# Memory projections at three quarters of the attention's pace, gating's first operands traced earlier

## The chip, the cores and the metric

The kernel runs on one core of a Trainium2 chip. The metric is device time in microseconds of one execution. An execution under the hardware profiler gives a trace, from which all views (page, windows, waits, chain, timeline) are taken. The engines are called PE (TensorE), DVE (VectorE), ACT (ScalarE), POOL (GpSimd) and SP (SyncE, which issues most loads and stores); PEld is TensorE's weight load.

## The reference, cut to what matters

One step of a hybrid decoder layer, in fp32, for a prompt of 1024 rows and for 8 samples with 8192 rows of paged cache each. The prompt goes through a mixer of two groups of heads (forgetting attention and a spatial gating unit), cross-attention into 256 memory tokens and a gated MLP; the samples go through the same weights against their caches. The parts that this change moves:

```python
def memory_kv(mem, g_mem, w_ck, w_cv):                 # "the memory's projections", 256 x 1024 each
    mn = rmsnorm(mem, g_mem)
    return mn @ w_ck, mn @ w_cv                        # then split into heads
def sgu_prompt(u, z, w_s, b_s):                        # "gating", chunks of 128 rows, 8 heads of 64
    mixed = einsum('hts,bcshd->bcthd', tril(w_s), zc) + b_s
    return u * mixed
...
xp = xp + merge_heads(fox_prompt(q, k, v, logf), sgu_prompt(u, z, w_s, b_s), g_att_out, g_sgu_out, w_o)
```

Gating's z comes normalised (a factor per row and one per column); its result gets an RMSNorm of its own before the merge. fp32 products of full precision are made as three products of split operands (`gemm3`, L272 to L274).

## The kernel before, in words

The prompt is worked in two halves of 512 rows. `p1` makes all input projections and writes q, k, v, u (`sgu_d`) and z (`zg_d`) to DRAM. Then come, for the first half, attention (`attention(0)`), for the second half attention (`attention(1)`), then for each half the merge, the output projection, cross-attention and the MLP.

Python generators set the order in which instructions are traced; each `yield` gives a rough cost. `mix(main, bg, ratio)` goes through `main`, adds `ratio` times the cost of each step to an account, and takes steps from `bg` as long as the account is positive. A decode generator for the samples is paced by the same costs (`PACE`, L76): one cache step per 12 units in the phase `att0`, one per 26 from the third head pair on (`attx`), one per 11 in `att1`. A cache step gathers a page of keys and of values (L1407, L1469), multiplies and reduces on DVE (L1414, L1415), and makes its value products on PE (L1475). The tracer's scheduler then places the instructions on each engine, and may move one ahead of others whose operands or buffers aren't ready in its own model; on the chip each engine runs its list in order.

`attention(0)` goes through four head pairs, each in two blocks of two row blocks for two heads: 8 score groups per pair, 32 in all (1.8 units each). A score group makes the scores (L798, L800, L802), the row maximum (L804) and the exponential (L805). Two groups later the probabilities are turned on PE (L827) and copied (L834) to a probability tile; after a block come the value products (`values`, L843) and the copy back (L852, L863, L865). The next pair is loaded (`load`, L724 to L731) and set up (`setup`, L741 to L783) in the second block of the pair before. At the last pair `late` (L1839) calls twice into `attention(1)`, whose first pair is thereby loaded and set up.

The filler beside it (`fill`, L1832) first gives `pmem` (L674): the memory's projections, 8 chunks of 5.2 units (24 products of 128 x 512 each, L272 to L274, and an evacuation, L711), with the weights loaded and split four at a time (L249, L235, L236). Then comes `gating(0)` (L618): `wst`, the masked chunk weights (L621, L622); for each of two pairs of row blocks the loads of z and u (L629, L630), z scaled (L632), 8 products on PE (L640), bias and product with u on DVE (L650), sums of squares on ACT (L661, which the profile shows at L230); then a reciprocal root (L663, shown at L222 and L223), the scaling (L669) and the store (L670). Each step of it is one unit.

One thing is scarce. `U` (L111) is a set of 18 buffers of 4 KB per partition, which holds all operands of attention, projections and gating: `pmem` keeps 4 (`mh`, `ml`), a head pair of the first half 5 (keys and values as loaded, and two tiles for each head), of the second half 7, gating 5 (`wst`, two z, two u), the probability tiles of a second block 2, attention's result 2. For the part that the change touches:

Of the kernel before, what the change touches and what calls it, by code (L numbers as in the profile page):

```python
# [49 lines left out]

NKV = 4
VLAG = 2
MIXR = 1.0
G0R = 0.0
WH = 5
WL = 4
WR = 4
# [21 lines left out]
def build(nc, tc, ctx, a, phases=None):  # L79
# [46 lines left out]
    def sm(shape, tag, bufs=2, dt=F32):  # L126
        return small.tile(shape, dt, tag=tag, bufs=bufs, name=nm(tag))
# [490 lines left out]
    def gating(hf):  # L618
        gsv = gains[0]
        wst = U([P, 8, P])  # L620
        nc.sync.dma_start(wst, a["wsT"])  # L621
        nc.vector.tensor_tensor(wst, wst, tri.unsqueeze(1).broadcast_to((P, 8, P)), op=ALU.mult)  # L622
        us_, ssu = [], sm([P, 4], "ssu", 1)
        for pr_ in range(2):
            z = U([P, 2, 512])
            u = U([P, 2, 512])
            t0 = hf * 4 + pr_ * 2
            rows = slice(t0 * P, (t0 + 2) * P)
            nc.sync.dma_start(z, zg_d[rows, :].rearrange("(c p) d -> p c d", p=P))  # L629
            nc.sync.dma_start(u, sgu_d[rows, :].rearrange("(c p) d -> p c d", p=P))  # L630
            for i in range(2):
                nc.vector.scalar_tensor_tensor(  # L632
                    z[:, i, :], z[:, i, :], rz[:, t0 + i : t0 + i + 1], gsv, op0=ALU.mult, op1=ALU.mult
                )
            yield 1
            for q in range(2):
                ps = BK()
                for j in range(4):
                    h = q * 4 + j
                    mmul(  # L640
                        ps[:, j * P : (j + 1) * P].rearrange("p (c d) -> p c d", d=64),
                        wst[:, h, :],
                        z[:, :, h * 64 : (h + 1) * 64],
                        start=True,
                        stop=True,
                    )
                for j in range(4):
                    h = q * 4 + j
                    uh = u[:, :, h * 64 : (h + 1) * 64]
                    nc.vector.scalar_tensor_tensor(  # L650
                        uh,
                        ps[:, j * P : (j + 1) * P].rearrange("p (c d) -> p c d", d=64),
                        gp[:, B_S + h : B_S + h + 1],
                        uh,
                        op0=ALU.add,
                        op1=ALU.mult,
                    )
                yield 1
            for i in range(2):
                with tc.issue_after(lastexp[0]) if lastexp else nullcontext():  # L660
                    ssq_into(ssu[:, pr_ * 2 + i : pr_ * 2 + i + 1], u[:, i, :])  # L661
            us_.append(u)
        r = rstd_of(ssu, AW, 4, "r4")  # L663
        yield 1
        for pr_ in range(2):
            u = us_[pr_]
            t0 = hf * 4 + pr_ * 2
            for i in range(2):
                nc.vector.tensor_scalar(u[:, i, :], u[:, i, :], r[:, pr_ * 2 + i : pr_ * 2 + i + 1], None, op0=ALU.mult)  # L669
            nc.sync.dma_start(sgn_d[t0 * P : (t0 + 2) * P, :].rearrange("(c p) d -> p c d", p=P), u)  # L670
        yield 1


    def pmem():  # L674
        rm = const.tile([P, 2], F32, tag="rm", name="rm")
        ssm = sm([P, 2], "ssm", 1)
        for mt in range(2):
            t = U([P, D])
            nc.sync.dma_start(t, a["mem"][mt * P : (mt + 1) * P, :])
            ssq_into(ssm[:, mt : mt + 1], t)  # L680
        r = rstd_of(ssm, D, 2, "r2")
        nc.vector.tensor_copy(rm, r)
        mh, ml = [], []
        for q in range(2):
            h, l = U([P, 4, 256], F32R), U([P, 4, 256], F32R)
            raw = WRAW(1024).rearrange("p (k m) -> p k m", m=256)
            nc.sync.dma_start(raw, a["memT"][q * 512 : (q + 1) * 512, :].rearrange("(k p) m -> p k m", p=P))
            for k in range(4):
                kk = q * 4 + k
                split(raw[:, k, :], h[:, k, :], l[:, k, :], scale=gp[:, G_MEM + kk : G_MEM + kk + 1])  # L690
            mh.append(h)
            ml.append(l)
        ahead = [wraw(wpair(a["w_ck"], kk, 0, 512), 1024) for kk in range(4)]
        before = newest(ENG.Activation)
        yield 0.1
        for w, dst in ((a["w_ck"], mk_d), (a["w_cv"], mv_d)):
            for n in range(2):
                with tc.issue_after(before):
                    ws = [wload(wpair(w, kk, n * 512, 512), 1024, ahead.pop(0) if ahead else None) for kk in range(4)]
                for mt in range(2):  # L700
                    ps = MM()
                    ms_ = slice(mt * P, (mt + 1) * P)
                    gemm3(
                        ps[:, :512],
                        [
                            (mh[k // 4][:, k % 4, ms_], ml[k // 4][:, k % 4, ms_], ws[k // 2][0][:, k % 2, :], ws[k // 2][1][:, k % 2, :])
                            for k in range(8)
                        ],
                    )
                    t = T2()  # L710
                    nc.scalar.activation(t, ps[:, :512], AF.Copy, scale=rm[:, mt : mt + 1])  # L711
                    nc.scalar.dma_start(dst[mt * P : (mt + 1) * P, n * 512 : (n + 1) * 512], t)
                    paused[0] = False
                    yield 5.2
# [1095 lines left out]
    def mix(main, bg, ratio):  # L1810

        t, more, res = 0.0, True, None
        while True:
            try:
                d = next(main)
            except StopIteration as e:
                res = e.value
                break
            yield d
            t += d * ratio  # L1820
            while more and t > 0:
                d = next(bg, None)
                more = d is not None
                if more:
                    t -= d
                    yield d
        if more:
            yield from bg
        return res

    def prompt():
        def fill():  # L1832
            yield from pmem()
            if not G0R:
                yield from gating(0)

        got, ahead = [], []
        att1 = attention(1, lambda: got.append(merge_in(0)))
        att0, fill0 = attention(0, (lambda: next(att1)) if LT < 4 else None, LT), fill()  # L1839

        def early():
            next(att0)
            next(fill0)

        yield from p1(early)
        phase[0] = "att0"
        att = yield from mix(att0, fill0, MIXR)
        def load_x(hf):
            xt = []
            for i in range(4):  # L1850
                t = U([P, D])
                nc.sync.dma_start(t, a["x"][(hf * 4 + i) * P : (hf * 4 + i + 1) * P, :])
                xt.append(t)
            return xt

        if LT > 3:
            yield next(att1)
        ending = close(0, att)
        next(ending)
        phase[0] = "att1"  # L1860
        ba_pool(True)
        if G0R:
            att = yield from mix(gating(0), att1, 1 / G0R)
        else:
            att = yield from beside(att1, ending, (0, 2))
        ba_pool(False)
        ending = close(1, att)
        next(ending)
        ends = []
        for hf in range(2):  # L1870
            if not got and hf == 0:
                got.append(merge_in(hf))
            xt = []
            phase[0] = f"mid{hf}"
            if hf == 0:
                mh, ml = yield from beside(merge(*got.pop()), ending, (3, 7))
            else:
                mh, ml = yield from ahead[0]
            if ends:
                yield from ends.pop()  # L1880
            sq = yield from out_proj(a["w_o"], mh, ml, xt, partial(load_x, hf))
            if hf == 0:
                ys = yield from mix(cross(xt, sq), gating(1), 0.05)
            else:
                ys = yield from cross(xt, sq)
            phase[0] = f"ffn{hf}"
            sq = yield from ffn(hf, xt, ys, (lambda: ahead.append(merge(*merge_in(1))) or ahead[0]) if hf == 0 else None)
            held[0] = False
            ends.append(final(hf, xt, sq))
        yield from ends.pop()  # L1890
# [121 lines left out]
```

## Time and profile before

| | us |
|---|---|
| median of 3 runs | 1818.56 (1815.97 to 1819.52) |
| profiled execution, its time | 1820.56 |
| its span in the trace | 1818.4 |
| PE busy | 1745.0 (96%) |
| DVE busy | 1397.5 (77%) |
| ACT busy | 734.4 (40%) |
| POOL busy | 510.0 (28%) |
| mean granted clock of TensorE | 0.986 of full speed |
| stage: first half's attention, projections, gating | 262.0 to 376.8 |

A window row gives the window, its length, the busy time of PE, PEld, DVE, ACT and POOL in it with instruction counts, the granted clock, the DMA engines' share and GB/s. A timeline row gives start, duration, engine, line, operation, output and inputs, and in brackets the idle time before it and what ended that. A wait row gives who waited for whom, total, times and the longest. A row of the chain gives start, duration and what the time went to. A row of a group gives line, engine, operation, operands and count, then busy time and the mean in ns of one, then idle time before them.

### The profile page before, as it was taken

The numbers are of one execution on the slowest core, as the hardware profiler recorded it, in microseconds if no ns is written. First come the engines' busy times: TensorE is split into PE (matmuls) and PEld (weight loads), VectorE is DVE, ScalarE is ACT, GpSimd is POOL, SyncE is SP. The second block draws the span as 40 slices with busy tenths as digits, with TensorE's granted clock in tenths as the row PEclk, the third lists the DMA queues.
The fourth block names the chain that finished last, engine by engine and source line by source line (L and its number), as shares of the span: only waits on it lengthen the run. The fifth ranks groups of instructions, "written<-read, shape, count | busy, mean of one in ns | idle before, by whom it ended". The sixth has DMA issues, their size and how long they took to land.

```text
span 1818.4 us, 25090 instructions
## 1 busy us (share of the span) xinstructions
PE 1745.0 (96%) x9637; PEld 1294.9 (71%) x9637; DVE 1397.5 (77%) x1729; ACT 734.4 (40%) x1378; POOL 510.0 (28%) x461
## 2 busy tenths in 40 slices
PE   8999999888998999999999999989899999999997
PEld 5887776656676767777777776766576778767775
DVE  4689668888788877999989899898875549845344
ACT  6332365455643544433333244235353324332332
POOL 1252334332133432223332333334222111011110
PEclk9999999899999999999999999989999999999999
DMA  8886889777696986679878779988787777568982
GB/s 295 306 297 231 302 297 329 242 266 224 219 398 257 342 310 260 257 285 340 316 279 311 271 306 340 381 300 324 290 309 290 267 268 265 179 266 289 359 314 82
DMA packets 157074, 521.06 MB, mean 287 GB/s; under 512 B 20874, under 2 KB 40842, under 8 KB 124186
## 3 DMA queue, kind: packets, MB, share of 16 engines
q0 software_dynamic: 57168, 341.14, 49.5%
q1 hardware_dynamic: 92874, 165.73, 26.4%
q10 hardware_dynamic: 6912, 12.59, 1.8%
q8 instruction: 76, 1.25, 0.3%
q14 instruction: 44, 0.36, 0.1%
HBM read 495.47 MB, written 23.93 MB: 286 GB/s over the span
## 4 chain that ended last, share of the span: by engine, by line
PE 72%; DMA 10%; issue 7%; DVE 6%; ACT 2%; POOL 2%; SPq 0%; POOLq 0%; DVEq 0%; ACTq 0%
PE ba L272 11%; PE ba L274 11%; PE ba L273 11%; PE bb L272 5%; PE bb L273 5%; PE bb L274 5%; PE dv L1475 5%; DMA kv<-cache_k,io 3%; DMA wr<-w_in 2%; DMA kv<-cache_v,io 1%; PE dv L321 1%; PE dv L1751 1%; PE ba L1056 1%; PE ba L1055 1%; PE ba L1057 1%
## 5 line engine op out<-in xcount | busy, mean ns | idle before, releaser
L235 ACT ACTIVATE wh<-wr 128x1024 fp32r<-128x1024 f32 (+2 forms) x220 | 228.9, 1044 | 489.2 <-PE ba L273 156.0
L236 DVE TENSOR_TENSOR wl<-wr,wh 128x1024 fp32r<-128x1024 f32 (+2 forms) x220 | 262.5, 1200 | 175.6 <-PE ba L274 65.7
L1407 POOL DMA_INDIRECT kv<-cache_k,io x128 | 205.6, 1606 | 551.2 <-DVE s L1427 318.9
L1423 DVE TENSOR_TENSOR kv<-kv,d 128x1024 f32<-128x1024 f32 (+1 forms) x156 | 258.0, 1681 | 35.1 <-DMA kv<-cache_k,io 35.1
L1427 DVE TENSOR_REDUCE s<-kv 128x16 f32<-128x1024 f32 (+1 forms) x156 | 258.2, 1674 | 0.1
L1469 POOL DMA_INDIRECT kv<-cache_v,io x128 | 165.3, 1291 | 282.8 <-PE dv L1475 191.8
L272 PE MATMUL ba<-u,wh 128*128 128x512 f32 (+1 forms) x560 | 220.3, 395 | 1.7 <-ACT u L238 1.7
L273 PE MATMUL ba<-u,wh 128*128 128x512 f32 (+1 forms) x560 | 220.2, 393 | 1.7 <-DVE u L239 1.5
L274 PE MATMUL ba<-u,wl 128*128 128x512 f32 (+1 forms) x560 | 219.5, 393 | 0.0
L272 PE MATMUL ba<-wh,u 128*128 128x512 f32 (+1 forms) x495 | 186.9, 379 | 0.9 <-ACT u L235 0.9
L273 PE MATMUL ba<-wl,u 128*128 128x512 f32 (+1 forms) x495 | 185.4, 375 | 1.2 <-DVE wl L236 1.2
L274 PE MATMUL ba<-wh,u 128*128 128x512 f32 (+1 forms) x495 | 183.8, 376 | 0.0
L272 PEld LDWEIGHTS ba<-u,wh 128*128 128x128 f32 x560 | 106.8, 191 | 30.6 <-issue 5.6
L273 PE MATMUL bb<-u,wh 128*128 128x512 f32 (+1 forms) x304 | 119.4, 393 | 9.2 <-DVE u L239 9.2
L274 PEld LDWEIGHTS ba<-u,wl 128*128 128x128 f32 x560 | 106.9, 191 | 29.1 <-issue 6.1
L273 PEld LDWEIGHTS ba<-u,wh 128*128 128x128 f32 x560 | 106.7, 191 | 27.5 <-issue 2.7
L1475 PE MATMUL dv<-kv,s 128*32 128x512 f32 x1024 | 124.2, 598 | 1.8 <-DMA kv<-cache_v,io 1.8
L272 PE MATMUL bb<-u,wh 128*128 128x512 f32 (+1 forms) x304 | 119.4, 393 | 0.0
L274 PE MATMUL bb<-u,wl 128*128 128x512 f32 (+1 forms) x304 | 118.6, 390 | 0.0
L272 PEld LDWEIGHTS ba<-wh,u 128*128 128x128 f32 x495 | 93.0, 188 | 26.0 <-issue 6.9
L274 PEld LDWEIGHTS ba<-wh,u 128*128 128x128 f32 x495 | 92.8, 188 | 21.5 <-issue 3.7
L273 PEld LDWEIGHTS ba<-wl,u 128*128 128x128 f32 x495 | 93.1, 188 | 19.7 <-DVE wl L236 1.9
(425 smaller groups left out, 3255.9 us busy)
## 6 DMA issues: line engine op xcount, KB each, us to landing
wr<-w_up SPq DMA_DIRECT2D x88, 512.0 KB
kv<-w_up POOLq DMA_DIRECT2D x22, 1024.0 KB, 8.0
wr<-w_down SPq DMA_DIRECT2D x40, 512.0 KB
kv<-w_down POOLq DMA_DIRECT2D x11, 1024.0 KB, 8.5
wr<-w_in SPq DMA_DIRECT2D x16, 512.0 KB
wr<-w_o SPq DMA_DIRECT2D x16, 512.0 KB
wr<-w_cq SPq DMA_DIRECT2D x16, 512.0 KB
wr<-w_co SPq DMA_DIRECT2D x16, 512.0 KB
```

The costliest lines, as they stand in the source:

```text
L235: nc.scalar.activation(h, src, AF.Copy)
L236: nc.vector.tensor_tensor(l, src, h.bitcast(F32), op=ALU.subtract)
L272: mmul(out, sh, mh, start=(i == 0), stop=False)
L273: mmul(out, sh, ml, start=False, stop=False)
L274: mmul(out, sl, mh, start=False, stop=(i == n - 1))
L321: mmul(ps[32 * j : 32 * j + 32, :w], xT[:, k, :] if nk == 8 else xT[:, k * 8 : k * 8 + 32], raw[:, q, j * w : (j + 1) * w], start=(k == 0) ...
L1055: mmul(pss[i], mh[k][:, tb], wh, start=(k == korder[0]), stop=False)
L1407: nc.gpsimd.indirect_dma_start(kv, None, a["cache_k"], off(kidx[:, b, ch : ch + 1]))
L1423: nc.vector.tensor_tensor(kvv[:, i : i + m, :], kvv[:, i : i + m, :], qb.unsqueeze(1).broadcast_to((P, m, 512)), op=ALU.mult)
L1427: nc.vector.tensor_reduce(s[:, ch * 4 + i : ch * 4 + i + m, :].rearrange("p k h -> p (k h)"), kvv[:, i : i + m, :].rearrange("p k (h d) -> ...
L1469: nc.gpsimd.indirect_dma_start(kv, None, a["cache_v"], off(kidx[:, b, ch : ch + 1]))
L1475: mmul(dv[32 * j : 32 * j + 32, :], s[:, ch * 4 : ch * 4 + 4, :].rearrange("p k h -> p (k h)"), kvv[:, j, :], start=(ch == 1), stop=(ch == ...
```

## The change

`MIXR` goes from 1.0 to 0.75, so that `mix` takes 0.75 units of filler for each unit of attention. `gating` is cut otherwise: loading and scaling a pair's operands becomes `inputs(pr_)`; the first pair's is traced with `wst` as its first step, the second pair's directly ahead of that pair's products, without a step between. `fill` takes that first step out of `gating(0)` after the seventh step of `pmem`, that is with two projection chunks still to come, and the rest after `pmem`'s end. The switch `G0R`, which was 0, is taken out with its branches. `gating(1)`, used beside cross-attention, gets the same new cut. Nothing is computed differently.

```diff
-MIXR = 1.0
-G0R = 0.0
+MIXR = 0.75
...
-        us_, ssu = [], sm([P, 4], "ssu", 1)
-        for pr_ in range(2):
+        ssu = sm([P, 4], "ssu", 1)
+        us_, zs_ = [], []
+        def inputs(pr_):
             z = U([P, 2, 512])
             u = U([P, 2, 512])
...
                 nc.vector.scalar_tensor_tensor(
                     z[:, i, :], z[:, i, :], rz[:, t0 + i : t0 + i + 1], gsv, op0=ALU.mult, op1=ALU.mult
                 )
-            yield 1
+            us_.append(u)
+            zs_.append(z)
+
+        inputs(0)
+        yield 1
+        for pr_ in range(2):
+            if pr_ == 1:
+                inputs(1)
+            z, u = zs_[pr_], us_[pr_]
             for q in range(2):
...
-            us_.append(u)
         r = rstd_of(ssu, AW, 4, "r4")
...
         def fill():
-            yield from pmem()
-            if not G0R:
-                yield from gating(0)
+            gate, n = gating(0), 0
+            for t in pmem():
+                n += 1
+                yield t
+                if n == 7:
+                    yield next(gate)
+            yield from gate
...
-        if G0R:
-            att = yield from mix(gating(0), att1, 1 / G0R)
-        else:
-            att = yield from beside(att1, ending, (0, 2))
+        att = yield from beside(att1, ending, (0, 2))
```

## The prediction

> **What bounds the kernel now.** I read the page first. TensorE is busy nearly throughout, so an edit can only gain where TensorE idles or runs below full clock. Then the table of windows, cut at the change's stage:
>
> ```profile
> PE 1745.0 (96%) x9637; PEld 1294.9 (71%) x9637; DVE 1397.5 (77%) x1729; ACT 734.4 (40%) x1378; POOL 510.0 (28%) x461
> ```
>
> ```profile
> 262.00:333.60 71.60, 69.89 (x387) 51.53 (x387) 60.45 (x101) 41.07 (x88) 28.95 (x35) 1.00 0.83 298
> 333.60:342.80 9.20, 7.04 (x52) 5.32 (x50) 6.28 (x16) 3.27 (x11) 3.18 (x5) 1.00 1.03 400
> 342.80:347.20 4.40, 0.04 (x1) 0.04 (x1) 2.80 (x9) 2.06 (x7) 0.00 (x0) 0.92 0.56 174
> 347.20:353.40 6.20, 6.20 (x29) 5.89 (x30) 4.37 (x11) 1.55 (x3) 1.21 (x2) 0.51 0.14 42
> 353.40:376.80 23.40, 18.56 (x127) 12.26 (x126) 19.23 (x42) 16.03 (x47) 12.63 (x18) 0.93 0.83 266
> ```
>
> The first half's attention begins at 262.0 us, the last memory projection ends at 333.6, the second half's attention starts at 376.8. The columns are length, busy time of PE, PEld, DVE, ACT and POOL, then granted clock, DMA share and GB/s. With projections beside it (first row) attention leaves TensorE idle for 71.6 - 69.9 = 1.7 us. After them, in 43.2 us, TensorE is busy for 7.04 + 0.04 + 6.20 + 18.56 = 31.8, idle for 11.4; 4.4 of these are one gap, after which the clock is 0.51 for 6.2 us (3.0 us lost) and 0.93 in the rest (0.07 x 18.56 = 1.3 lost).
>
> The list of TensorE's waits names the gap, and the chain of waits says what lies behind it:
>
> ```profile
> PE bb L640 <- DVE u L632: 4.4, 1, 4.4
> PE ba L640 <- DVE u L632: 0.6, 1, 0.6
> ```
>
> ```profile
> 295.66 18.74 DMA u<-o_k
> 330.81 14.86 DMA u<-zg_d
> 359.66 2.01 DMA ks_d<-u
> 366.29 9.43 DMA sgn_d<-u
> ```
>
> The long wait is for gating's **second** operands: z of its second pair of row blocks, issued at 330.8 and landed 14.9 us later. The **first** operands, those that the change brings forward, cost 0.6 us.
>
> **What decides when a load may go out.** The 18 buffers of `U` are all taken here. I compared issue times with the ends of earlier users:
>
> ```profile
> 315.17 0.39 PE L800 MATMUL ba<-u,u 68*128 68x512 f32 x1
> 326.37 0.40 PE L800 MATMUL ba<-u,u 68*128 68x512 f32 x1
> ```
>
> ```profile
> 315.62 0.34 SPq L621 DMA_DIRECT2D u<-wsT  x1
> 316.02 0.43 SPq L629 DMA_DIRECT2D u<-zg_d  x1
> 326.81 0.37 SPq L630 DMA_DIRECT2D u<-sgu_d  x1
> 327.35 0.37 SPq L730 DMA_DIRECT2D u<-o_k  x1
> 330.81 0.37 SPq L629 DMA_DIRECT2D u<-zg_d  x1
> ```
>
> ```profile
> 333.87 0.56 POOL L750 DMA_DIRECT2D u<-cq_d  x1 [4.12 <-PE bb L274]
> 368.45 0.56 POOL L762 DMA_DIRECT2D u<-ck_d  x1 [0.39 <-PE ms L843]
> 380.21 0.54 POOL L750 DMA_DIRECT2D u<-cq_d  x1 [8.12 <-DMA sgn_d<-u]
> ```
>
> A pair of buffers falls free when a head's last scores end (315.5, 326.8); `wst` with the first z go out at once at the first, the first u with the next head pair's keys at the second. The second z goes at 330.8, halfway through the last projection chunk, when half of its `mh` and `ml` are done with. Counting buffers in program order (4 of the projections, 2 results, 5 per head pair, 1 per probability tile, 5 of gating) gives 18 at each of these points, and every release goes to the request that is next in program order. So I take it that buffers are handed out in the order of the program, though the loads themselves are ready long before.
>
> **The change, part by part.** Counted from the code, attention has 74.6 units of work, projections 41.6, gating 8 (after: 7). At ratio 1 the last projection chunk comes after 16 of 32 score groups, at 0.75 after 22.
>
> *More cover.* In the trace 14 score groups run after the projections:
>
> ```profile
> L798 PE MATMUL ba<-u,u 128*128 128x384 f32 (+3 forms) x14 | 6.2, 444 | 0.0
> ```
>
> Their loss without the gap and its slow clock is 11.4 - 4.4 + 1.3 = 8.3 us, 0.6 each. After the change 10 are left: 4 x 0.6 = 2.4 us less; the covered stretch grows by four groups at its own loss of 2.4% (1.7 of 71.6), about 0.3. **Gain 2.1.**
>
> *The gap at its present place* goes, as the second operands are now traced in the last head pair: 4.4 + 3.0 = **7.4**. The first operands' 0.6 lies in the 8.3 already. Their three SP issues, 1.1 us in the rows above, are moved ahead of the second half of w_cv on SP. Those weights went out 27.9 us ahead of use, which covers it:
>
> ```profile
> 289.88 5.60 SPq L249 DMA_DIRECT2D wr<-w_cv  x4
> ```
>
> ```profile
> 317.77 0.48 PE L272 MATMUL ba<-wh,u 128*128 128x512 f32 x1
> ```
>
> If that cover went, the 10.4 us for which SP stood at L630 would be the price.
>
> *What is late next.* In the changed program the second half's set-up (`late`, called at the last head pair's start) asks for 7 buffers before `inputs(1)` asks for 2. Ahead of the second z then stand one buffer of the last head pair's set-up, 2 probability tiles and these 7: 10. Until the last head pair the releases are 2 (the third pair's first head), 4 (projections), 2 (its second head) and 1 (the first z): 9. So the second z and u wait for the next release, the third head pair's last `values` (L843), which also released L762 above. Here is that point beside the last pair's first and last scores, and the second attention's first probability tile:
>
> ```profile
> 360.49 0.46 PE L798 MATMUL ba<-u,u 128*128 128x128 f32 x1
> 366.62 1.73 PE L843 MATMUL ms<-u,u 128*64 128x256 f32 x14
> 372.47 0.48 PE L798 MATMUL ba<-u,u 128*128 128x512 f32 x1
> 384.64 0.59 ACT L834 ACTIVATE u<-bb 128x512 f32<-128x512 f32 x1
> ```
>
> I call the first of these S. `values` ends at S + 7.9, attention's scores at S + 12.5, the second attention's first probability tile is written at S + 24.1. Gating's chain from there needs these rows:
>
> ```profile
> 340.41 2.05 PE L640 MATMUL ba<-u,u 128*128 128x128 f32 x16 [0.57 <-DVE u L632]
> ```
>
> ```profile
> L632 DVE SCALAR_TENSOR_TENSOR u<-u,rz,xg 128x512 f32<-128x512 f32 x4 | 2.8, 746 | 1.6 <-DMA u<-zg_d 1.6
> L650 DVE SCALAR_TENSOR_TENSOR u<-bb,gp,u 128x128 f32<-128x128 f32 x4 | 1.1, 345 | 0.8 <-PE bb L640 0.8
> L230 ACT ACTIVATE junk<-u 128x512 bf16<-128x512 f32 x4 | 2.5, 626 | 0.0
> L230 ACT ACTIVATION_READ_ACCUMULATOR junk<-u 128x1 f32 x4 | 0.8, 193 | 0.0
> L223 POOL TENSOR_TENSOR r4r<-r4r,mhalf 128x4 f32<-128x4 f32 x1 | 1.0, 1045 | 0.1
> L669 DVE TENSOR_SCALAR u<-u,r4r 128x512 f32<-128x512 f32 x4 | 1.7, 479 | 0.0
> ```
>
> The load's landing isn't known for the new time: between 2.0 (`ks_d`) and 18.7 (`o_k`). I take 9.4, that of `sgn_d`, also 512 KB from SP and in the same uncovered stretch; the same for the store at the end. Then S + 7.9 + 9.4 + 2 x 0.75 (L632) + 2.05 (L640) + 4 x 0.345 (L650) + 2 x 0.82 (squares) + 1.0 (POOL; the small DVE step left out) + 1.7 (L669) + 9.4 (store) = S + 36.0. By the same count the buffers of the second attention's first probability tiles come from this store (before, its next head pair waited for it, 380.21 above). Behind ACT's waiting L834 stand its exponentials, and TensorE waits for those. The entry is 36.0 - 24.1 = **11.9 later** against S. For a slow clock after a gap of this kind I add half of 3.0, **1.5**, since set-up transposes may break the gap; the bounds are 0 and 3.0.
>
> *Decode.* Fewer units come before the pace falls from one step per 12 to one per 26: 7.43 steps instead of 8.0.
>
> ```profile
> L1475 PE MATMUL dv<-kv,s 128*32 128x512 f32 x1024 | 124.2, 598 | 1.8 <-DMA kv<-cache_v,io 1.8
> ```
>
> A step has 124.2 / 128 = 0.97 us of TensorE; 0.57 of one moves into later, fuller stages: **+0.6** (0 if it meets idle time).
>
> **Sum:** -2.1 - 7.4 + 11.9 + 1.5 + 0.6 = **+4.5 us**. The profiled execution took 1820.56 us (span 1818.4), the runs' median is 1818.56 (1815.97 to 1819.52), so I apply it to the median: **1823**. With both transfers at 2.0 the entry is no later and the sum is -8.9; with both at 18.7 it is some 23. One of the two at the 14.9 of the second z, or as much sooner than 9.4, gives this case's own range, 1817.5 to 1828.5.
>
> [...] After the gap of 4.4 us the row shows a clock of 0.51. [...]
>
> **The rivals.** *Second operands in time:* buffers are handed to whoever is ready, and the second z goes out when the last projection's four buffers fall free, well ahead of use. Then nothing runs late: -2.1 - 7.4 + 0.6 = -8.9, of which I keep -7 because the covered stretch holds more attention for DVE: **1811.5**. For it: the loads have no other condition, and traffic is thinner once projections are spread. Against: `wst` waited until 315.6 although it was ready. It decides if the second z lands before the last head pair's second score group.
>
> *The gap only moves:* the operands are late, but probability tiles get other buffers. The gap costs 7.4 at its new place as at the old one: -2.1 + 0.6 = -1.5, **1817**. That would also be the case that the change doesn't do what it says for the time: sooner first operands meet a wait of 0.6 us.
>
> **How the numbers follow.** Forecast 44%, operands in time 34%, the gap moves 22%. Faster by over 0.2% (3.6 us, about what a measurement of this kernel can tell from no change) takes 32 of the second case and 3 of the third: 0.35. Slower takes 40 of the first and 3 of the third: 0.43. Same is the rest, 0.22. The range 1809 to 1829 covers the second case down to -8.9 and the first case's own range, and leaves out its ends with two slow or two fast transfers and a gain in the second case beyond its sum.
>
> **What would show it.** Right: in the changed profile the second `zg_d` load goes out after the last `values` of the third head pair, L640's wait stands among the last scores or behind them, and L834 at the second attention's start waits for the `sgn_d` store. Wrong: the second `zg_d` load goes out as the projections end and L640 doesn't wait; or L834 goes ahead of the store. The cover is shown by fewer than 14 score groups after the last projection. Decode's gathers would run half a step later from there on.

## The result and the profile after

The changed kernel takes **1827.17 us** (median of 6 runs, 1824.74 to 1828.37) against 1817.31 (6 runs, 1814.22 to 1819.52) for the kernel before: ratio **1.0057**, 95% interval 1.0044 to 1.0070. It is slower by 9.9 us. The profiled execution took 1828.13 us, its span is 1826.4, 8.0 longer than before.

The lines of the changed kernel stand up to 8 away from those of the kernel before: gating's products are L648 (L640 before), the split products L271 to L273, scores L805 (L798), turning L834 (L827), the copy to a probability tile L841 (L834), `values` L850 (L843), the split copies L238 (L239), decode's key multiply L1430 (L1423).

Page, busy time by engine: TensorE makes the same 9637 products and is busy as long (1744.6 against 1745.0), and the mean clock is the same (0.985 against 0.986). So the 8 us are idle time on the whole, though single stretches run slower or faster than before.

```profile
PE 1744.6 (96%) x9637; PEld 1293.3 (71%) x9637; DVE 1396.4 (76%) x1725; ACT 737.3 (40%) x1380; POOL 489.9 (27%) x461
```

The windows of the changed stage. The last projection ends at 348.6, the last head pair's first scores (the prediction's S) begin at 352.35, the second attention at 382.61:

```profile
261.30:348.60 87.30, 81.70 (x449) 59.07 (x448) 67.54 (x113) 49.07 (x112) 36.82 (x47) 0.98 0.80 280
348.60:354.00 5.40, 5.26 (x43) 4.53 (x41) 4.62 (x14) 4.16 (x10) 1.67 (x3) 1.00 0.80 261
354.00:358.80 4.80, 0.00 (x1) 0.03 (x1) 4.56 (x9) 2.67 (x9) 2.20 (x4) 0.84 0.90 289
358.80:364.00 5.20, 4.32 (x19) 2.06 (x19) 0.65 (x3) 0.38 (x1) 0.52 (x1) 0.50 0.03 11
364.00:369.04 5.04, 0.00 (x1) 0.00 (x1) 1.42 (x2) 0.38 (x1) 0.00 (x0) 0.50 0.76 237
369.04:374.00 4.96, 4.96 (x24) 4.87 (x25) 2.05 (x8) 0.28 (x1) 0.00 (x0) 0.50 0.01 3
374.00:382.70 8.70, 7.62 (x50) 4.80 (x49) 6.98 (x20) 8.03 (x25) 2.27 (x3) 0.98 0.21 62
```

Where before there was one gap of 4.4 us with 6.2 us at a clock of 0.51 behind it, there are now two, of 4.8 and 5.0, and TensorE's 4.32 + 4.96 = 9.3 us of work behind them all run at 0.50. TensorE's waits in 340:392 name both gaps:

```profile
PE bb L648 <- DVE u L632: 5.0, 1, 5.0
PE ms L1454 <- DVE pm L1448: 4.8, 1, 4.8
```

The first is gating's wait for its second operands, at its new place. The second was not there before: decode's softmax (L1448, L1454) comes due ahead of the third head pair's `values`, and DVE, whose reduction it waits for, is busy for 4.56 of these 4.80 us. The timeline says how the one leads to the other:

```profile
356.19 0.46 ACT L812 ACTIVATE t<-ba,mx 128x256 f32<-128x256 f32 x1
358.80 0.37 PE L1454 MATMUL ms<-cp,pm 128*8 128x128 f32 x1 [4.82 <-DVE pm L1448]
359.54 3.26 PE L850 MATMUL ms<-u,u 128*64 128x256 f32 x16 [0.37 <-DVE m L1457]
363.09 0.52 POOL L769 DMA_DIRECT2D u<-ck_d  x1 [6.84 <-PE ms L850]
363.39 0.54 SPq L629 DMA_DIRECT2D u<-zg_d  x1
364.02 0.42 SPq L630 DMA_DIRECT2D u<-sgu_d  x1
367.57 1.42 DVE L632 SCALAR_TENSOR_TENSOR u<-u,rz,xg 128x512 f32<-128x512 f32 x2 [7.65 <-DMA u<-zg_d]
369.04 2.08 PE L648 MATMUL bb<-u,u 128*128 128x128 f32 x8 [5.04 <-DVE u L632]
370.91 0.42 PE L834 MATMUL bb<-cp,t 128*128 128x128 f32 x1
372.69 0.45 PE L805 MATMUL ba<-u,u 128*128 128x128 f32 x1
383.16 1.15 SPq L677 DMA_DIRECT2D sgn_d<-u  x2
390.39 0.60 ACT L841 ACTIVATE u<-bb 128x512 f32<-128x512 f32 x1 [0.93 <-issue]
```

`values` ends at 359.54 + 3.26 = 362.8, and only then do L769, the second z and the second u go out. The z has landed by 367.57, some 4.2 us after its issue. L648 waits 5.04 us for it and starts at 369.04, and what follows on TensorE starts behind it: a turning (L834, at 370.91) of probabilities that were written by 356.7, and the last pair's remaining scores (from 372.69).

**The lag along the kernel.** To see where 8 us come from I compared the start of the same instruction in both traces (changed minus before): the second attention's first scores, and the first product of each of the four output projections (L1055 in the kernel before: the mixer's and cross-attention's, for each half), then the last split product. All kernels of this study, one profiled execution each:

| us later than before at | second attention | mixer's output, half 1 | cross's output, half 1 | mixer's output, half 2 | cross's output, half 2 | last product | median, ratio |
|---|---|---|---|---|---|---|---|
| kernel before, time | 376.9 | 497.1 | 651.8 | 1135.3 | 1295.5 | 1808.7 | |
| after | +5.8 | +5.7 | +15.4 | +18.8 | +9.9 | +8.0 | 1.0057 |
| A ratio alone | +13.3 | +11.2 | +16.3 | +15.4 | +11.8 | +11.2 | 1.0091 |
| B cut alone | -8.6 | -5.9 | +9.2 | +7.8 | +7.0 | +7.9 | 1.0078 |
| C second operands sooner | -3.4 | -0.3 | +8.5 | +8.9 | +1.5 | +1.8 | 1.0047 |
| D old cut in half 2 | +7.2 | +6.4 | +16.5 | +14.8 | +8.0 | +6.5 | 1.0099 |
| E after, decode ahead | +4.7 | +5.3 | +9.0 | +18.1 | +11.9 | +10.8 | 1.0111 |
| F before, decode behind | -1.6 | -0.7 | +0.2 | +3.3 | +11.8 | +9.4 | 1.0081 |
| G B, one unit | -8.1 | -2.5 | +0.9 | +11.0 | +21.7 | +18.8 | 1.0081 |
| H C, decode ahead | -0.9 | +2.1 | +5.6 | +8.9 | +5.0 | +5.3 | 1.0049 |
| I cut of half 1, old account | -8.4 | -8.2 | -12.0 | -13.7 | -14.1 | -14.1 | 0.9955 |
| J I with the ratio | +5.6 | +6.8 | +3.0 | +4.6 | +2.3 | +2.4 | 1.0025 |

Two things limit what the table can say. E has the changed kernel's program up to the second attention, F that of the kernel before, G that of B and H that of C, and their starts there differ from those by 1.1, 1.6, 0.5 and 2.5 us; so a difference of a stage under some 3 us says nothing. And the last column is not the ratio: the profiled execution of the kernel before took 3.2 us more than the median of its runs, D's 7.5 less than that of its own, those of E and F 3.7 less, G's 3.8 more.

In the changed kernel the entry costs 5.8, the first half's middle stage another 9.7 (5.7 to 15.4), and the second half's gives 8.9 back (18.8 to 9.9). My prediction had the first of these only. In the first half's cross-attention TensorE's waits (552:602) hold

```profile
PE bb L272 <- DVE u L238: 8.4, 3, 6.5
```

against, at the same place in the kernel before (545:597),

```profile
PE bb L273 <- DVE u L239: 3.2, 3, 2.1
```

That is 5.2 of the 9.7 us. DVE's timeline shows what stands ahead of the copies that TensorE waits for: a multiply of decode's keys, for whose page DVE waits 1.90 us:

```profile
559.97 0.87 DVE L238 SCALAR_TENSOR_TENSOR u<-ba,gp,u 128x256 fp32r<-128x256 f32 x2
562.75 2.36 DVE L1430 TENSOR_TENSOR kv<-kv,d 128x1024 f32<-128x1024 f32 x2 [1.90 <-DMA kv<-cache_k,io]
565.02 0.48 DVE L238 SCALAR_TENSOR_TENSOR u<-ba,gp,u 128x256 fp32r<-128x256 f32 x1
```

So two theories stood after the result. **Entry:** buffers are handed out in program order, the second operands come late, and the rest is a consequence of the time of arrival. **Decode's place:** both the ratio and the new cut change how many units pass before each pace sets in, so decode's steps fall elsewhere in the later stages, and that moves the time by itself.

### The profile page after: what moved, and what is told of

Read it like the earlier page. It is cut to its first block, busy times and chain, and to the rows that moved or that the text cites. A ratio compares the mean times of both kernels' runs of the same rounds, so it can differ in the third digit from the quotient of the medians.

```text
span 1826.4 us, 25085 instructions
## 1 busy us (share of the span) xinstructions
PE 1744.6 (96%) x9637; PEld 1293.3 (71%) x9637; DVE 1396.4 (76%) x1725; ACT 737.3 (40%) x1380; POOL 489.9 (27%) x461
## 4 chain that ended last, share of the span: by engine, by line
PE 62%; issue 5%; DMA 4%; DVE 3%; ACT 2%; POOL 1%; POOLq 0%; DVEq 0%; ACTq 0%; SPq 0%
PE ba L271 9%; PE ba L272 9%; PE ba L273 9%; PE bb L273 5%; PE bb L272 5%; PE bb L271 5%; PE dv L1482 5%; DMA kv<-cache_v,io 1%; PE dv L320 1%; PE dv L1758 1%; DMA kv<-cache_k,io 1%; DMA u<-an_d 1%; PE ba L1062 1%; PE ba L1064 1%; PE ba L1063 1%
## 5 line engine op out<-in xcount | busy, mean ns | idle before, releaser
L235 DVE TENSOR_TENSOR wl<-wr,wh 128x1024 fp32r<-128x1024 f32 (+2 forms) x220 | 262.2, 1199 | 156.1 <-PE ba L273 62.4
L1414 POOL DMA_INDIRECT kv<-cache_k,io x128 | 176.1, 1376 | 593.3 <-DVE s L1434 397.7
L1430 DVE TENSOR_TENSOR kv<-kv,d 128x1024 f32<-128x1024 f32 (+1 forms) x158 | 260.5, 1677 | 36.3 <-DMA kv<-cache_k,io 36.3
L1476 POOL DMA_INDIRECT kv<-cache_v,io x128 | 170.1, 1329 | 279.8 <-PE dv L1482 219.9
L271 PE MATMUL ba<-u,wh 128*128 128x512 f32 (+1 forms) x560 | 220.0, 394 | 4.0 <-ACT u L237 3.3
L272 PE MATMUL ba<-u,wh 128*128 128x512 f32 (+1 forms) x560 | 219.5, 392 | 1.7 <-DVE u L238 1.7
L273 PE MATMUL ba<-u,wl 128*128 128x512 f32 (+1 forms) x560 | 218.4, 391 | 0.0
L271 PE MATMUL ba<-wh,u 128*128 128x512 f32 (+1 forms) x495 | 187.0, 380 | 2.9 <-ACT u L234 1.7
L272 PE MATMUL ba<-wl,u 128*128 128x512 f32 (+1 forms) x495 | 186.2, 377 | 1.7 <-DVE wl L235 1.7
L273 PE MATMUL ba<-wh,u 128*128 128x512 f32 (+1 forms) x495 | 184.1, 377 | 0.0
L271 PEld LDWEIGHTS ba<-u,wh 128*128 128x128 f32 x560 | 105.9, 189 | 34.9 <-issue 7.3
L272 PE MATMUL bb<-u,wh 128*128 128x512 f32 (+1 forms) x304 | 118.5, 390 | 12.7 <-DVE u L238 12.7
L272 PEld LDWEIGHTS ba<-u,wh 128*128 128x128 f32 x560 | 106.0, 189 | 34.1 <-issue 9.4
L273 PEld LDWEIGHTS ba<-u,wl 128*128 128x128 f32 x560 | 106.0, 189 | 28.1 <-issue 5.2
L271 PE MATMUL bb<-u,wh 128*128 128x512 f32 (+1 forms) x304 | 118.2, 389 | 0.5 <-ACT u L237 0.5
L273 PE MATMUL bb<-u,wl 128*128 128x512 f32 (+1 forms) x304 | 117.7, 388 | 0.0
L271 PEld LDWEIGHTS ba<-wh,u 128*128 128x128 f32 x495 | 93.3, 189 | 27.7 <-issue 6.9
L272 PEld LDWEIGHTS ba<-wl,u 128*128 128x128 f32 x495 | 93.5, 189 | 20.2 <-DVE wl L235 2.8
L273 PEld LDWEIGHTS ba<-wh,u 128*128 128x128 f32 x495 | 93.1, 189 | 20.6 <-issue 3.7
```

The lines of the kernel that those rows point to most:

```text
L235: nc.vector.tensor_tensor(l, src, h.bitcast(F32), op=ALU.subtract)
L271: mmul(out, sh, mh, start=(i == 0), stop=False)
L272: mmul(out, sh, ml, start=False, stop=False)
L273: mmul(out, sl, mh, start=False, stop=(i == n - 1))
L1414: nc.gpsimd.indirect_dma_start(kv, None, a["cache_k"], off(kidx[:, b, ch : ch + 1]))
L1430: nc.vector.tensor_tensor(kvv[:, i : i + m, :], kvv[:, i : i + m, :], qb.unsqueeze(1).broadcast_to((P, m, 512)), op=ALU.mult)
```

## The experiments

Ratios are to runs of the kernel before on the same chip. Edits are made in the changed kernel where nothing else is said. "Account" is the sum of units that decode's pace draws on.

**A and B: each part alone.** A is the kernel before with the new ratio, B the changed kernel with the old one.

```diff
-MIXR = 1.0
+MIXR = 0.75
```

> The kernel before with the ratio 0.75 alone (gating and its place as before, all after the last projection chunk). Theory (the last head pair's set-up of the second half takes the buffers that gating's second operands need, and gating's end runs into the second attention): gating is now traced wholly behind the last projection, so its second z goes out later still; a wait at L640 of 4 to 8 us and a start of the second attention 4 to 8 us after that of the kernel before; total 1821 to 1830. Rival (the new cut of gating is what costs): no wait longer than before, total 1812 to 1818.

A: 1833.38 us (1828.60 to 1838.34), ratio 1.0091 (1.0068 to 1.0114). The waits are as long as expected, but there are two, and the start and the time lie beyond the range. With all of gating behind the projections, both operands are waited for, and between the two requests lie 19 us (SP's issues, then TensorE's waits, of A):

```profile
349.55 0.43 SPq L629 DMA_DIRECT2D u<-zg_d  x1
368.64 0.53 SPq L629 DMA_DIRECT2D u<-zg_d  x1
```

```profile
PE ba L640 <- DVE u L632: 5.4, 1, 5.4
PE bb L640 <- DVE u L632: 4.7, 1, 4.7
```

> The changed kernel with the ratio back at 1.0: new cut of gating and its first step two chunks before the projections' end. Theory: projections end before the last two head pairs, their four buffers come free well before the second half's set-up asks, so the second z goes out about 331 us as before and the wait stays near 4.4 us; the second attention starts within 2 us of the kernel before; total 1814 to 1822. Rival (the cut costs): about the changed kernel's 1827.

B: 1829.48 us, ratio 1.0078 (1.0056 to 1.0100). The time is the rival's. Its second z goes out during the projections, as expected, but no wait of gating's for it follows, and the second attention starts 8.6 us sooner than before:

```profile
332.81 0.37 SPq L629 DMA_DIRECT2D u<-zg_d  x1
```

So the new cut gains at the entry, which I had not expected, and the ratio loses there: it alone makes the entry 13.3 late, and beside the cut it moves it from 8.6 sooner to 5.8 later. But B is slower than the kernel before all the same: it loses 15 us between the mixer's output and cross's output of half 1 (-5.9 to +9.2). Entry alone can't be the reason.

**C: the second operands asked for when gating resumes,** ahead of `late`'s seven requests.

```diff
         inputs(0)
         yield 1
+        if hf == 0:
+            inputs(1)
         for pr_ in range(2):
-            if pr_ == 1:
+            if pr_ == 1 and hf:
                 inputs(1)
```

> The changed kernel with the first half's second operands requested when gating resumes after the projections, ahead of the second half's set-up; gating of the second half as changed. Theory (buffers are handed out in program order): the second z goes out as the projections end, about 349 us, and not after the third head pair's last value products (363.4 in the changed kernel); the wait at L648 falls from 5.0 to under 1 us, the second attention starts 5 to 9 us sooner than in the changed kernel. Total 1816 to 1822 if the rest stays, since 2 to 10 us of the loss lie in cross-attention of the first half. Rival (the stall is the decode's softmax before it, a wait of 4.8 us on DVE): the start moves by under 2 us.

C: 1824.49 us (11 runs, 1819.05 to 1830.50), ratio 1.0047 (1.0033 to 1.0062). SP's issue and TensorE's longest wait there, of C:

```profile
345.56 0.37 SPq L629 DMA_DIRECT2D u<-zg_d  x1
```

```profile
PE bb L650 <- ACT junk L229: 3.9, 1, 3.9
```

Only the place in the program changed, and the second z goes out 17.8 us sooner (363.39 in the changed kernel), as an order of buffers by the program would have it. The wait for z is gone, the other wait (decode's softmax) too, with gating's products now ahead of it in TensorE's list (357.44 and 361.26), and one of 3.9 is left. The second attention starts 9.2 sooner than in the changed kernel. The time hardly falls, and misses the expected range: the ratio is 1.0047 against 1.0057, with overlapping intervals. This kernel too loses 9 us behind the mixer's output.

**D: the old cut in the second half's gating,** which is worked beside cross-attention.

```diff
-        inputs(0)
-        yield 1
+        if hf == 0:
+            inputs(0)
+            yield 1
         for pr_ in range(2):
-            if pr_ == 1:
+            if hf:
+                inputs(pr_)
+                yield 1
+            elif pr_ == 1:
                 inputs(1)
```

> The changed kernel with the old cut for the second half's gating alone, which runs beside cross-attention of the first half. Theory A (the loss of some 10 us in cross-attention of the first half comes from where decode's DVE work meets the turning of the rows, not from gating's cut): total within 3 us of the changed kernel's 1827, or any change comes with another position of decode. Theory B (the new cut costs there): the wait of 6.5 us at the turning goes, total 1817 to 1820.

D: 1834.17 us, ratio 1.0099 (1.0076 to 1.0122), slower than the range of either theory; it also gives decode back the unit of the second half's cut. The loss in the middle stage stays (+6.4 to +16.5), and so does the wait at L272 (8.3, the longest 6.4): in this kernel it isn't due to gating's new cut beside cross-attention.

**E to H: decode moved by itself.** Going through the generators with the paces shows that at the first half's middle stage decode is 0.55 of a step behind in the changed kernel (4.4 units at a pace of 8) and 1 unit behind in B. E adds the 4.4 to the changed kernel, F takes 4.4 from the kernel before, G adds 1 to B, H adds 4.4 to C:

```diff
             phase[0] = f"mid{hf}"
+            if hf == 0:
+                acc[0] += 4.4
```

> The changed kernel with 4.4 units added to decode's account where the first half's middle stage begins, which makes good the 0.55 of a step (4.4 units at a pace of 8) that decode is behind there. Theory (decode's place): the changed kernel's loss of 13 us in front of the first cross-attention arises because decode's page multiply now stands ahead of DVE's copies of the transposed rows, and TensorE waits 6.5 us for them. Then that wait goes, the lag at the first cross-attention's first scores falls from +18.5 to +6 to +10. If the second half's middle stage then gives nothing back, the end stays at +6 to +8 (1824 to 1827 us); if it still gives back its 8, the end is at 0 or below (1815 to 1818). Rival (the later arrival, or the traffic, not decode's place): the lag there stays at +16 to +20 and the time at 1825 to 1828.

> The kernel before with 4.4 units taken from decode's account at the same place, so that decode stands there as in the changed kernel. Theory (decode's place): a wait of several us for DVE's copies appears in front of the first cross-attention, its scores come 8 to 14 us late, and the second half's middle stage gives part of it back: 1819 to 1827 us. Rival: it arrives at the old time, so nothing is lost there: 1815 to 1819.

> The new cut with the old ratio, and one unit added to decode's account at the same place, which makes good the one unit that the new cut has fewer. Theory (decode's place): the 13 us that the cut alone loses in front of and in the first cross-attention shrink to under 5, and with the 8.6 us gained at the second attention's entry the time is 1810 to 1820. Rival: the loss there has another cause (in this kernel TensorE's list has the second half's gating in it, with a wait of 4.2 us that no releaser is named for), and the time stays at 1826 to 1831.

> The changed kernel with the first half's second operands asked for ahead of the second attention's buffers, and with 4.4 units added to decode's account where the middle stage begins. Theory (decode's place): the lag at the first cross-attention's scores falls from +13.9 to +2 or less, and the time from 1824.5 to 1812 to 1820. Rival: both stay, 1822 to 1827.

E: 1834.73 us, ratio 1.0111 (1.0083 to 1.0140). F: 1833.65, 1.0081 (1.0058 to 1.0103). G: 1835.47, 1.0081 (1.0054 to 1.0108). H: 1826.27, 1.0049 (1.0031 to 1.0067). By their times the theory's expectations failed: F alone came out slower as expected, but by more than expected (1819 to 1827) and by a loss at another place; H's time is the rival's. Stage by stage it is otherwise. From the mixer's output to cross's output of half 1 the lag grows by 3.7 us in E (9.7 in the changed kernel), by 3.4 in G (15.1 in B) and by 3.5 in H (8.8 in C): in each of these pairs the place of decode's steps sets most of this loss. TensorE's waits of E in the same window:

```profile
PE bb L272 <- DVE u L238: 4.6, 2, 3.8
```

It is not decode's place alone, though. F leaves decode where the changed kernel has it and loses only 0.9 in this stage. And in B the long wait is not at the split copies, but at the second half's gating, whose scaling (L632) ends at 566.13 on DVE behind two of decode's reductions; L648 starts at 566.23 (TensorE's waits of B, the whole stage):

```profile
PE ba L648 <- issue: 4.2, 1, 4.2
PE bb L272 <- DVE u L238: 3.6, 3, 1.7
```

But E then loses 9.1 up to the second half's mixer, G 10.1 there and 10.7 in the second half's cross-attention. And F, in which nothing of the change is present, loses nothing in the first half and 8.5 us in the second half's cross-attention. Its waits there, by who waited (1202:1307):

```profile
DVE kv L1423 <- DMA kv<-cache_k,io: 11.9, 4, 6.5
ACT cbs L1175 <- DVE cmx L1172: 16.7, 4, 7.3
PE ba L1170 <- ACT u L1178: 8.5, 1, 8.5
```

The first two in the kernel before (1199:1296); the third is not there:

```profile
DVE kv L1423 <- DMA kv<-cache_k,io: 8.6, 4, 4.8
ACT cbs L1175 <- DVE cmx L1172: 7.4, 2, 5.3
```

In program order the three belong together: DVE stands at a decode multiply for its page, the softmax's maxima (L1172) come late, ACT's exponentials (L1175, L1178) behind them, and TensorE's next scores wait for the buffers. That they are one chain is read from the lines, not shown wait by wait. What F does show: **half a decode step, moved alone, costs the kernel before 0.8%** (0.6 to 1.0), as much as the whole change (0.4 to 0.7) or more.

**Decode taken out of the later stages.** Both kernels once more, with decode's remaining steps, and the samples' work behind them, done after the prompt:

```diff
+    off = [False]
...
             phase[0] = f"mid{hf}"
+            off[0] = True
...
-        while bgs and not held[0] and most and acc[0] >= PACE[phase[1] or phase[0]]:
+        while bgs and not held[0] and not off[0] and most and acc[0] >= PACE[phase[1] or phase[0]]:
```

> The kernel before, with decode taken out of everything from the first half's middle stage on and done after the prompt instead, with the single-token work behind it. Everything up to the end of the second attention is as in the kernel before. It is the base for the next run and much slower than the kernel before, by some 200 us or more. Read by the start of the prompt's stages: the second attention's start within 2 us of the kernel before.

> The changed kernel with decode taken out in the same way. Theory (the change itself costs its entry, the rest of the gains and losses is decode's place beside the later stages): it starts the second attention 5 to 8 us later than the kernel before and keeps that to the prompt's end; at each later stage the lag to the base stays within 4 us of that, and the whole differs from the base by +3 to +9 us. Rival (the change itself has a second cost in the first half's middle stage): the lag grows there by 9 us or more, as with decode beside it, and the whole differs by +12 or more.

Before: 2482.76 us. Changed: 2490.22. The two ratios to the kernel before, 1.3659 (1.3635 to 1.3682) and 1.3693 (1.3662 to 1.3724), overlap in their intervals, so the whole doesn't tell them apart, though the medians differ by 7.5 us, as expected. Their traces do: the changed one is later by 8.4 us at the second attention, 3.4 at the mixer's output of half 1, 4.0 at cross's, 1.9 at both of half 2, and 0.7 at the prompt's last split product. Without decode beside it the change shows no second loss in the middle stage, and its entry is made good behind it but for 0.7 us. My expectation that the lag is kept to the end failed; the rival, a cost of the change's own in the middle stage, failed too.

**I and J: the same account, with and without the ratio.** I has the new cut in the first half alone (D's edit), the old ratio, and, in the first half, the unit that the new cut saves added to gating's last step, so that decode's account is that of the kernel before from the second attention on. J is I with the new ratio, and with 5.2 units added where the second attention begins, so that the account is that of the kernel before from the middle stage on.

```diff
-        yield 1
+        yield 1 if hf else 2
```

```diff
-MIXR = 1.0
+MIXR = 0.75
...
         phase[0] = "att1"
+        acc[0] += 5.2
```

> The new cut in the first half alone, with the old ratio and the old cut in the second half, and with one unit added to the gating unit's last step, so that decode's account is that of the kernel before at every later stage. Theory (the cut with the old ratio gains 8 at the entry, and decode's place decides whether it is kept): the second attention starts 6 to 9 us sooner, no more than 5 are lost in the first half's middle stage, and the time is 1807 to 1817 us. Rival (the stages behind are tuned to the arrival in time too, so an arrival 8 us sooner loses as much as a place that is moved): 1818 to 1830 us.

> The kernel of the run before (new cut in the first half alone, decode's account of the kernel before) with the changed kernel's ratio of 0.75, and 5.2 units added to decode's account where the second attention begins, which makes good what the ratio takes from decode in the first attention. From the first half's middle stage on its account is that of the kernel before, so it differs from the run before by the ratio alone. It starts the second attention 5 to 7 us later than the kernel before, as the changed kernel does. Theory (with decode in its old place the later stages cost what they did): that lag goes on or shrinks to the end, 1817 to 1824 us. Rival (the stages behind are tuned to the time of arrival too): another 5 us or more are lost behind it, 1825 to 1840 us.

I: **1808.53 us** (1806.44 to 1811.39), ratio **0.9955** (0.9938 to 0.9971), faster than both kernels, as expected. Its stage (first from the second z's request to the last pair's first scores, then on to the second attention's first) has no slow clock (1.00 in both rows) and no wait of gating's:

```profile
332.00:352.70 20.70, 17.36 (x125) 13.82 (x124) 19.77 (x47) 11.93 (x36) 7.64 (x13) 1.00 0.78 267
352.70:368.50 15.80, 12.68 (x98) 8.08 (x96) 13.63 (x31) 10.81 (x33) 8.95 (x12) 1.00 0.93 300
```

The 8.4 us are kept to the end: 8.0 by the medians. (The 14.1 of the table is between single executions: I's took 2.1 us less than its median, that of the kernel before 3.2 more.) J: 1823.06 us (11 runs, 1819.98 to 1825.44; before 1819.26), ratio 1.0025 (1.0016 to 1.0034), in the range of the theory. It has the changed kernel's two gaps (TensorE's waits of J):

```profile
PE bb L652 <- DVE u L632: 4.9, 1, 4.9
PE ms L1458 <- DVE pm L1452: 4.8, 1, 4.8
```

With decode where it was, J's entry of +5.6 shrinks to +2.4 (3.8 by the medians), against +8.0 in the changed kernel (9.9). I and J differ by the ratio, with decode's account the same from the middle stage on: the ratio costs 14.0 us at the second attention and, by the medians (-8.0 and +3.8), 11.8 in the whole. J and the changed kernel differ by decode's account and the second half's cut.

## Why the prediction was right in its sign, and where its reasons failed

The forecast was 1823.0 with a range of 1809 to 1829; 1827.17 lies in it, near its upper end. The sum was +4.5 us; it came out as +8.0 between the profiled spans and +9.9 between the medians.

- **The gains (2.1 and 7.4).** The gap left its old place, 9 score groups follow the projections (10 predicted, 14 before), and S came at 352.35 instead of 360.49, 8.1 sooner; 0.8 of that was there when the first attention began, so 7.3 belong to the change. Predicted 9.5. Right, a little large.
- **Buffers in program order, the second operands behind `late`.** Right to the instruction: the second z goes out behind the third pair's last `values` and next to L769. C moves the request and the issue follows by 17.8 us.
- **The entry, 11.9 later, and 1.5 for the clock.** The second attention's first probability tile is written at 390.39, S + 38.0; predicted S + 36.0 and 1.5 for the clock, before S + 24.1. The sum, 13.4 against 13.9, is right, its terms are not. The landing is 4.2, not 9.4. The 9.4 of the store aren't paid at all: the copy L841 at 390.39 starts when the turning ahead of it ends (the row below: 389.70 + 0.61 = 390.31), so "L834 waits for the store" did not come true. In their place stand decode's softmax (4.8, not foreseen), the wait for z with the last scores behind it (5.0) and the slow clock (half of 9.3 us, 4.6, beyond my bound of 3.0, since I had one gap in mind and there are two). That set-up transposes in a gap would spare the clock, my ground for half of 3.0, no run shows; here the clock stood at 0.50 from 358.00 to 374.00. That the sum came out is luck: the errors cancelled.

```profile
389.70 0.61 PE L834 MATMUL bb<-cp,wr 128*128 128x128 f32 x4
```

- **Decode, +0.6: the step that failed.** The place was right (0.55 of a step, predicted 0.57), the price wrong: I priced a step by its TensorE time. F shows half a step at 0.8% of the kernel before. In its place stand waits of a DVE list that holds decode's page waits and reductions (6.5 us at once in front of the first cross-attention), and their size and sign differ from stage to stage.
- **What the sum left out.** It had no term for the second half's gating, which got the same cut. E and J have the same ratio, nearly the same entry (+4.7 and +5.6) and decode made good at the first half's middle stage; J has the old cut in half 2, and so its unit, and stands 3.8 us above the kernel before where E stands 17.0 above it. D has that cut without the account and is slower than the changed kernel. So the two act together, as far as these runs tell: J makes decode good from the second attention on, E from the middle stage on, and whether the cut counts by its order or by its missing unit was not tried.
- **That an entry's loss goes on to the end.** The sum took it for granted. Without decode beside the later stages 8.4 becomes 0.7; with decode in its old place 5.6 becomes 2.4 (3.8 by the medians).

With decode and the second half held as they were, J, the time is +3.8 us (1.0025), close to the sum of +4.5. That is the part that I had reasoned about, though its terms met by luck here too. The other some 6 us of the 9.9 come with decode's account and the second half's cut, and I hadn't seen them. The rivals: "second operands in time" (1811.5) is what the cut does at the old ratio, I at 1808.5; the ratio that comes with it in this change rules it out. "The gap only moves" (1817) has the right picture, but counts one gap where there are two.

Three things stay open. The runs of E and G spread over 14 and 17 us, those of D and F over 12 (those of I and J over 5), which was not explained; a stage's loss read from one profiled execution of them is rougher than their ratio. E, G and H have the same account and the same code from the first half's middle stage on, yet from the mixer's output of half 1 to the last product E loses 5.5 us, G 21.3 and H 3.2; their times of arrival, or that spread, must make the difference, and no run tells which. And more buffers, which would end the competition between gating and `late`, were not tried.

## What to carry to other kernels

Where a second stream of work is paced by a count of the first, a change of the count moves the stream in all later stages: hold its place fixed when you measure an edit, or you measure both. Read from the program order who gets a scarce buffer next; a load that was traced behind seven other requests went out 17.8 us later here than ahead of them. And price a moved step by what stands behind its waits in the engines' lists, not by its own busy time: 0.55 of a step that has 0.97 us of TensorE cost the kernel before 0.8% here.

## What the runs showed of the hardware

How long TensorE's granted clock stayed near 0.5 behind a gap differed from gap to gap. In the kernel before one gap of 4.4 us was followed by 6.2 us of unbroken work at 0.51, and then by 1.00 in 353.40:354.00. A has two gaps, of 5.4 and 4.7 us; behind the first TensorE worked for 4.96 us without a break at 0.50, behind the second for 3.64 at 0.51, and after each its clock was 1.00 (in 364.34:369.74 and in 378.06:380.00):

```profile
359.38:364.34 4.96, 4.96 (x23) 4.88 (x23) 2.61 (x11) 0.03 (x1) 0.00 (x0) 0.50 0.37 150
374.42:378.06 3.64, 3.64 (x17) 3.64 (x18) 1.52 (x6) 0.00 (x0) 0.00 (x0) 0.51 0.00 0
```

In the changed kernel the clock fell within the gap of 4.8 us (0.84 over its window) and came back behind the second gap's work:

```profile
356.00:357.00 1.00, 0.00 (x0) 0.00 (x0) 0.94 (x3) 1.00 (x5) 0.25 (x1) 1.00 0.79 295
357.00:358.00 1.00, 0.00 (x0) 0.00 (x0) 0.97 (x2) 0.35 (x2) 0.00 (x0) 0.65 1.04 385
358.00:358.80 0.80, 0.00 (x1) 0.03 (x1) 0.65 (x1) 0.00 (x0) 0.00 (x0) 0.50 0.56 223
374.00:375.00 1.00, 1.00 (x6) 0.37 (x4) 1.00 (x5) 0.57 (x3) 0.00 (x0) 0.82 0.00 0
375.00:377.00 2.00, 2.00 (x15) 1.53 (x15) 1.14 (x4) 2.00 (x8) 0.00 (x0) 1.00 0.01 4
```

Between these rows it was 0.50 throughout: in the 5.2 us behind the first gap (4.3 of them busy), in the gap of 5.0 and in the 5.0 us of unbroken work behind that. By an estimate from these rows the two gaps cost some 4.6 us by the slow clock (half of 9.3 us of work), against 3.0 for the one gap before (0.49 of 6.2). What the clock's return depends on, these runs do not tell.
